# Pads between the SBUF tiles of the second block of an f32 transformer kernel on one Trainium2 core

## The chip, the core and the metric

The kernel runs on one core of a Trainium2 chip. Five engines share the work: TensorE (PE, matmuls; PEld is its loading of weights), VectorE (DVE), ScalarE (ACT), GpSimd (POOL) and SyncE (SP, which issues most DMAs). Tiles lie in SBUF, 128 partitions wide; a tile's place is one byte address, the same in each partition. Matmul results go to PSUM. The metric is the device time of one execution in microseconds (us); smaller is better.

## What is computed

Two blocks, one after the other, on 512 tokens with 1024 features, all in f32. The first (modulated norms, a gated delta rule, a window attention, a mixture of 32 experts) is not touched by the change. The second is:

```python
f = swiglu(rms_norm_2(h, ffn1_norm_pre), ffn1_w_gate, ffn1_w_up, ffn1_w_down)   # 1024 -> 2816 -> 1024
h = h + 0.5 * rms_norm_2(f, ffn1_norm_post)

proj = rms_norm_2(h, mix_norm_pre) @ w_in            # q, k, v (12 heads of 128), xr, yr, gates
q, k, v, xr, yr, gl = jnp.split(proj, splits, axis=-1)
attn = ...    # three dilated window attentions, merged by their log-sum-exp
rec = rg_lru_branch(xr, ...) * jax.nn.gelu(yr)       # conv of width 4, gates, a scan over the tokens
gates = jax.nn.sigmoid(gl).reshape(B, S, 2, D_MODEL)
merged = gates[:, :, 0] * (attn @ w_attn_branch) + gates[:, :, 1] * (rec @ w_rec_branch)
h = h + rms_norm_2(merged @ w_out, mix_norm_post)

f = swiglu(rms_norm_2(h, ffn2_norm_pre), ffn2_w_gate, ffn2_w_up, ffn2_w_down)
h = h + 0.5 * rms_norm_2(f, ffn2_norm_post)
```

## The kernel before

Activations are kept transposed: features on the partitions, the 512 tokens along a partition, so eight tiles of 2 KB per partition (`x0` to `x7`) hold all 1024 features. A projection `W^T x` gives 128 features at a time: eight k-tiles of weights, 128x128 each (512 bytes per partition, one after the other in one weight tile of 4 KB), against the eight activation tiles.

A large product is made of three f32r products. Each operand is split into a head of few bits and an exact rest, `h + l`, and `mm3` (L262 to L270) adds W_h x_h, W_h x_l and W_l x_h in PSUM:

```python
for i, k in enumerate(kts):
    w1, w2 = wh[:, i * P:(i + 1) * P], wl[:, i * P:(i + 1) * P]
    mm(ps, w1, xh[k], ...)      # L268
    mm(ps, w1, xl[k], ...)      # L269
    mm(ps, w2, xh[k], ...)      # L270
```

So a weight tile means 24 matmuls, each with its own load of 128x128 weights and 512 columns of activations that stream through; the loads run beside the matmul before. Weights come raw from HBM (`wload`, tile `wraw`); `wsplit` makes the head `wh` on ScalarE (L255) and the rest `wl` on VectorE (L256). `wraw`, `wh` and `wl` have four buffers each in the pool `wp2`; a new load waits until TensorE has done with a buffer.

The second block (`block2`) runs in this order:

- `ffn`, twice (before and after the mixer): `enter` closes the layer before and makes the first projections by halves of the tokens (256 columns); then gate and up projections from `xh`/`xl` (512 columns); their results are split to `hh`/`hl` in the pool `f1` (`f2`) and go through the down projections; `close` makes the last projections, the first four with 512 columns, the last four by halves with 256. `posth` (L1546) is a small tile of gains at the start of that pool.
- `mixer2`: four rounds, each with nine projections for one head of each attention group, then one head of the recurrence (`lru`: products by `xh`/`xl`, and small ones by `ch`/`cl`), into which the steps of `attention` (fp32 matmuls on `f` tiles, `sc`, `pT`) are woven. Then the merge: gates from `xh`/`xl`, the attention branch from `ah`/`al`, the recurrent one from `f`/`rs` (L1782 on), and `close` with `mh`/`ml`.

The order of the instructions on each engine follows the program text and a few woven generators; no table sets it. A tile's address follows from the pools: a pool lays its tiles one behind the other in the order in which tags are first used, and pools stand on each other like a stack.

Of the kernel before, what the change touches and what calls it, by code (L numbers as in the profile page):

```python
# [16 lines left out]
PSUM = bass.MemoryType.PSUM  # L17
# [13 lines left out]
# --------------------------------------------------------------------------  # L31
# host side: layout of the inputs and constants that depend on shapes alone
# --------------------------------------------------------------------------
def _mt(w, cols=None):
    """[K, M] -> [M/128, 128 (k), K/128, 128 (m)]"""
    if cols is not None:
        w = w[:, cols]
    k, m = w.shape
    return np.ascontiguousarray(w.reshape(k // P, P, m // P, P).transpose(2, 1, 0, 3))


def _cols(v):
    """[n*128] -> [128, n]"""
    return np.ascontiguousarray(np.asarray(v).reshape(-1, P).T)


def layout(a):
# [39 lines left out]
    # block 2  # L87
# [23 lines left out]
    def lru(n):  # L111
        w = a[n][0].reshape(4, 2, P, 2, P)  # head, k tile, k, m tile, m
        return w.transpose(2, 0, 3, 1, 4).reshape(P, 8 * 2 * P)
# [15 lines left out]
def constants():  # L129
# [8 lines left out]
    # [t, c]: t <= c / t > c inside a chunk  # L138
# [31 lines left out]
    # relative position: one-hot bucket rows and a mask row, over u  # L170
# [14 lines left out]
# --------------------------------------------------------------------------  # L185
# device side
# --------------------------------------------------------------------------
# [5 lines left out]
def weave(main, *fill):  # L193
    """the steps of main, and after each one `rate` steps of every filler (gen, rate)"""
    due = [0.0] * len(fill)
    for _ in main:
        for i, (gen, rate) in enumerate(fill):
            due[i] += rate
            while due[i] >= 1.0:
                due[i] -= 1.0  # L200
                next(gen, None)


class Net:
# [16 lines left out]
    def bt(self, shape, dt=F32):  # L221
        """a 2 KB per partition tile out of the shared set"""
        return self.t(self.bp, shape, "big", dt, bufs=self.nbig)
# [22 lines left out]
    # ---- weights: raw f32 -> 12-bit head (f32r) + exact rest (f32r)  # L246
# [11 lines left out]

    def weights(self, ap, n):
        return self.wsplit(self.wload(ap, n), n)  # L260

    def mm3(self, ps, wh, wl, xh, xl, kts, start=True, stop=True):  # L262
        """ps += W^T x over the k-tiles; wh/wl [128, nk*128]; xh/xl lists of [128, N]"""
# [8 lines left out]
    def mm3y(self, ps, wh, wl, xh, xl, kts, start=True, stop=True, n=3):  # L272
        """mm3 in steps of n k-tiles"""
# [10 lines left out]
    # ---- rsqrt of a small tile (x > 0), Newton on the vector engine  # L284
# [11 lines left out]
    # ---- softplus of a small tile  # L296
# [20 lines left out]
    # ---- 1/rms over the features of a T-layout activation, broadcast to all partitions  # L317
    def sumsq(self, acc, k, src):
        """acc += src^2"""
# [7 lines left out]
    def sumsq2(self, acc, k, src, hs):  # L327
        """acc[:, hs] += src[:, hs]^2, without the tensor engine or the vector engine"""
# [7 lines left out]
    def rstd_half(self, hf, *accs):  # L336
        """[P, 2]: 1/rms of the tokens of a half; the sums over the features on the tensor engine"""
# [36 lines left out]
    # ---------------------------------------------------------------- block 1  # L374
    def ada(self, items, raws=None):
        """mod[:, g] = w_ada^T silu(c) + b_ada by halves: the k-tiles as moving operand in four column tiles"""
# [49 lines left out]
    def block1(self):  # L426
# [39 lines left out]
        # statistics of x  # L466
# [5 lines left out]
        # scale1, shift1 by halves; k-tiles 0..3 of the projections of k follow the first halves  # L472
# [50 lines left out]
        # conv + silu (twice the value)  # L523
# [14 lines left out]
        def stats2(src, pst, base):  # L538
            """pst[:, i, base:base+2] = per token sums of squares over the two 64-halves"""
# [10 lines left out]
        # ---- gates  # L550
        def gates():
            # four k-tiles beside each other in the columns of the array
# [23 lines left out]
        def decays():  # L576
# [4 lines left out]
            # sum over a chunk, per head on the partitions of its half  # L581
# [12 lines left out]
        # ---- k: token major, normalised, and back  # L594
# [32 lines left out]
        # ---- decay and -M, its transpose  # L627
# [30 lines left out]
        # ---- q, v  # L658
# [11 lines left out]
        # ---- attention inside chunks, transposed, over k  # L670
# [19 lines left out]
        # ---- projections of the window attention  # L690
# [46 lines left out]
        # ---- sliding window attention  # L737
# [59 lines left out]
        # ---- z  # L797
# [7 lines left out]
        # ---- (I + M)^-1 by doubling of the diagonal blocks  # L805
# [46 lines left out]
        # ---- scaled v and k, token major, behind the inverse  # L852
        vb, kd, nw = MT, kt, [None] * 4

        def uw():
# [11 lines left out]
            for i in range(4):  # L867
# [3 lines left out]
                # -w^T [d (head parity), pair, chunk parity * 64]  # L871
# [11 lines left out]
        # ---- scan over the chunks; o = s o', s = rq / 8: s rsqrt(s^2 mean(o'^2) + eps)  # L883
# [62 lines left out]
        # results of the experts: rows for the first and the second expert of a token  # L946
# [7 lines left out]
        # ---- output projection: the rows of the window attention, then those of the delta rule  # L954
# [14 lines left out]
        # router: logits = (x * rstd * gain + shift) W = rstd * (x (gain W)) + shift W  # L969
# [34 lines left out]
    # ------------------------------------------------- block 1: mixture of experts  # L1004
    def moe(self):
# [5 lines left out]
        # the pairs of one group at a distance: its experts tend to be in demand together  # L1011
        order = [4 * g + i for i in range(4) for g in range(4)]
        NP = NE // 2
        # the results of the last pairs go to x by the tensor engine, the others by DRAM
        NL = 2

        def load(n, part=(0, 1)):
            """weights of pair n: gate | up in two halves per expert, down"""
# [15 lines left out]
        # slots beyond the last token keep finite values  # L1034
# [4 lines left out]
        # ---- normalized tokens, token-major, and a copy in DRAM  # L1039
# [13 lines left out]
        # ---- routing  # L1053
# [3 lines left out]
        def first_max(l, n, tag):  # L1057
            """the maximum, one-hot of its first place"""
# [24 lines left out]
        # [tok, tile, expert]  # L1083
# [10 lines left out]
        # tokens of the same expert before a token: in its tile, and in the tiles before (last: all)  # L1094
# [7 lines left out]
        # place of a token at its experts, from 1  # L1102
# [9 lines left out]
        # weights of the two experts  # L1112
# [20 lines left out]
        # pair: token, weights at its two experts, rows of the results  # L1133
# [6 lines left out]
        # tiles of the passes beyond the first  # L1140
        q1, q2, q3, q4 = (self.t(self.tp, [P, S], "cy" if q < 2 else "th") for q in range(4))
        # (no reuse of an index that a transfer may still read)
# [3 lines left out]
        def oindex(p, r):  # L1146
            """place of a slot's row in yd, or its token (the last pairs); its token"""
# [14 lines left out]
        def select(p, r):  # L1162
            """slots 64r..64r+63 of the two experts of the p-th pair: one-hot by token; token and weight of a slot"""
# [19 lines left out]
        def gather(p, r):  # L1183
            """their tokens, one on a partition"""
# [8 lines left out]
        def feed(xTs, hf, pt):  # L1193
            """gain and shift of the tokens, features on the partitions"""
# [19 lines left out]
        def pick(oh):  # L1214
            """the same by the tensor engine, without the way through DRAM"""
# [11 lines left out]
        def piece(p, c, o, r):  # L1227
            """512 columns of the weights of an expert of pair p"""
# [30 lines left out]
        def expert2(p, hT, idx, wv, r=0):  # L1259
            """weighted results, to DRAM; of the last pairs: in two parts, with the one-hot of the tokens by slot"""  # L1260
# [23 lines left out]
        def combine(ys, hs):  # L1284
            """x += gate * the results of the slots, at their tokens"""
# [13 lines left out]
        def ahead(p):  # L1299
            """the passes of pair p beyond the first: tokens fetched early"""  # L1300
# [11 lines left out]
        def more(p):  # L1312
            """the second and third pass of pair p"""
# [9 lines left out]
        def rest(p, r=3):  # L1323
            """the passes beyond, with weights loaded again"""
# [5 lines left out]
        def fetch(i):  # L1330
            """the results in DRAM for the tokens of a tile"""
# [5 lines left out]
        def collect(i, y):  # L1337
            """x += gate * the results in DRAM"""
# [51 lines left out]
    def headmm(self, aT, bT, i):  # L1390
        """[c, h, s] = sum_d a[d, c] b[d, s] for the two chunks of pair i; even heads, odd heads"""
# [24 lines left out]
    # ---------------------------------------------------------------- block 2  # L1416
    def bias_tables(self):
        """rows of the relative bias (with the mask), repeated in DRAM to be read back skewed"""
# [20 lines left out]
    def bias_load(self, dst, j, p):  # L1439
        """dst [128, 512]: group 0 (256 keys), group 1, group 2 (128 keys of the phase)"""  # L1440
# [9 lines left out]
    def halfsplit(self, h, l, src):  # L1450
        """h + l = src / 2"""
# [3 lines left out]
    def addnorm(self, k, f, pb, gcol, hs):  # L1455
        """x += f * gain / rms(f) for a half of the tokens (pb: 1/rms, in PSUM)"""
# [4 lines left out]
    def close(self, f, aps, xh, xl, evac):  # L1461
        """the last projections of a layer, f[m] = evac(W[m]^T x); the last four of them by halves of the tokens"""
# [27 lines left out]
    def enter(self, aps, gcol, post=None):  # L1490
        """the end of a layer (post: its result, 1/rms of the halves and gain) and the first projections of the next:
        xh + xl = x * gcol; returns the projections with the weights aps and 1/rms of x, broadcast"""
# [47 lines left out]
    def ffn(self, wgu, wd, pre, postg, post, fp):  # L1540
        """the projections down; returns what enter() needs to close the layer"""
# [3 lines left out]
        ph = self.t(fp, [P, KT], "posth")  # L1545
# [39 lines left out]
    def attention(self, j, q, k, vt, ap2, o):  # L1585
        """the p phases of head j, in steps"""
# [61 lines left out]
    def lru(self, rb, lp, rec):  # L1648
        """the gated recurrence, a head after the other, in steps"""
        nc, v, s = self.nc, self.nc.vector, self.nc.scalar  # L1650
        A, c2 = self.A, self.cols2
        cb, bx, ba, apar = (c2[:, 8 * i:8 * i + 8] for i in (6, 7, 8, 9))
        convw = self.const("convw2", [P, KT, 4], pool=lp)
# [8 lines left out]
        def head(h):  # L1662
# [17 lines left out]
            for q in range(2):  # L1680
                # twice gelu(yr)
# [43 lines left out]
    def mixer2(self, post):  # L1725
# [3 lines left out]
        with tc.tile_pool(name="mx", bufs=1, reuse_waits="tile") as mx:  # L1729
            att = [self.t(mx, [P, S], f"rs{k}") for k in range(4)]  # L1730
            rec = [self.t(mx, [P, S], f"rs{k + 4}") for k in range(KT)]
            with tc.tile_pool(name="at", bufs=1, reuse_waits="tile") as ap2:
                head = self.lru(rb, ap2, rec)
                for j in range(4):
# [27 lines left out]
            with tc.tile_pool(name="mg", bufs=1, reuse_waits="tile") as gp:  # L1762
                ah = [self.t(gp, [P, S], f"ah{k}", F32R) for k in range(4)]
                rh = [self.t(self.ap, [P, S], f"f{k}", F32R) for k in range(KT)]
                # a rest takes the place of the result before it
# [54 lines left out]
    def build(self):  # L1820
# [6 lines left out]
        with ExitStack() as st:  # L1827
# [31 lines left out]
            with ExitStack() as s1:  # L1859
# [5 lines left out]
                self.wp = pool(s1, "wp2", 4, reuse_waits="tile")  # L1865
                self.nsplit = 4
# [22 lines left out]
```

## Time and profile before

| | before |
|---|---|
| runs, median of 3 | 2241.49 us (2240.81 to 2242.68) |
| profiled execution, span from first to last instruction | 2238.9 us |
| TensorE busy | 2095.0 us, 94% |
| VectorE busy | 1078.0 us, 48% |
| ScalarE busy | 718.2 us, 32% |
| GpSimd busy | 202.9 us, 9% |
| second block | 857 to 2239 us of the span |

Of the profiled execution the page gives the span, not its time as a run; the span stands 2.6 us below the median of the runs. A matmul's record lasts longer than the distance to the next one's start, because matmuls are pipelined; a run's rate is read from the starts. Rows of the trace carry the names of the tiles without buffer numbers: `mm<-xh,wh` is a matmul into the PSUM tile `mm` with the moving operand `xh` and the weights `wh`.

### The profile page before, as it was taken

How to read it: one execution, taken by the hardware profiler on the slowest of the kernel's cores; microseconds unless marked ns; L12 is line 12 of the kernel's file. 1: busy time of each engine (PE TensorE's matmuls, PEld its weight loads, DVE VectorE, ACT ScalarE, POOL GpSimd, SP SyncE). 2: the span in 40 equal slices, each digit the busy share in tenths (PEclk: the TensorE clock that was granted, in tenths of full speed). 3: DMA queues.
4: the chain of work that ended last, by engine and by line, in shares of the span. 5: the costliest groups of instructions: out<-in, count | busy, mean ns of one | idle time of the engine just before them, and what ended most of it. 6: DMA issues, size and time to landing. Idle time of an engine off the chain costs nothing.

```text
span 2238.9 us, 32214 instructions
## 1 busy us (share of the span) xinstructions
PE 2095.0 (94%) x12908; PEld 1567.7 (70%) x12908; DVE 1078.0 (48%) x2071; ACT 718.2 (32%) x1197; POOL 202.9 (9%) x223
## 2 busy tenths in 40 slices
PE   5999999788888978999999899999999999999996
PEld 3677677553333427888888787878878888888886
DVE  4663655542221227553354864746564447542444
ACT  3432442122222224322222443525452243222221
POOL 3020002011111122000001300000000031000002
PEclk9999999788999988999999999999999999999998
DMA  7343315075968962323332232323222322233321
GB/s 262 112 133 105 105 48 160 29 284 215 399 238 329 382 249 95 99 90 91 102 92 82 88 83 76 113 67 113 62 99 90 108 76 81 93 89 95 98 90 38
DMA packets 93877, 294.53 MB, mean 132 GB/s; under 512 B 15746, under 2 KB 27010, under 8 KB 81404
## 3 DMA queue, kind: packets, MB, share of 16 engines
q1 hardware_dynamic: 86364, 278.03, 36.4%
q0 software_dynamic: 7328, 14.01, 1.9%
q8 instruction: 119, 1.95, 0.4%
q14 instruction: 66, 0.54, 0.1%
HBM read 286.12 MB, written 20.23 MB: 137 GB/s over the span
## 4 chain that ended last, share of the span: by engine, by line
PE 57%; DVE 3%; POOL 1%; ACT 1%; issue 1%; POOLq 0%; ACTq 0%; DVEq 0%
PE mm L269 18%; PE mm L270 18%; PE mm L268 18%; PE sm L1605 1%; DVE xl L1507 1%; PE mm L1633 1%; POOL x L1459 1%; POOL ss L334 1%; DVE cy L1458 0%; PE mm L1630 0%; ACT wh L255 0%; PE sm L1620 0%; PE sm L1757 0%; PE mm L1289 0%; PE sm L1603 0%
## 5 line engine op out<-in xcount | busy, mean ns | idle before, releaser
L268 PE MATMUL mm<-xh,wh 128*128 128x512 f32 (+1 forms) x1584 | 621.4, 395 | 8.4 <-ACT xh L1506 4.1
L269 PE MATMUL mm<-xl,wh 128*128 128x512 f32 (+1 forms) x1584 | 612.4, 387 | 4.0 <-DVE xl L1507 4.0
L270 PE MATMUL mm<-xh,wl 128*128 128x512 f32 (+1 forms) x1584 | 609.7, 386 | 0.1
L255 ACT ACTIVATE wh<-wraw 128x1024 fp32r<-128x1024 f32 (+3 forms) x282 | 274.1, 974 | 771.8 <-PE mm L269 681.4
L256 DVE TENSOR_TENSOR wl<-wraw,wh 128x1024 fp32r<-128x1024 f32 (+3 forms) x282 | 315.0, 1118 | 196.6 <-ACT wh L255 191.3
L268 PEld LDWEIGHTS mm<-xh,wh 128*128 128x128 f32 x1584 | 301.4, 191 | 81.5 <-issue 8.3
L269 PEld LDWEIGHTS mm<-xl,wh 128*128 128x128 f32 x1584 | 303.1, 191 | 66.1 <-DVE xl L1507 5.7
L270 PEld LDWEIGHTS mm<-xh,wl 128*128 128x128 f32 x1584 | 302.6, 191 | 62.9 <-issue 1.2
L334 POOL TENSOR_TENSOR ss<-ss,sq 128x256 f32<-128x256 f32 (+1 forms) x69 | 66.9, 970 | 951.6 <-ACT sq L333 935.5
L268 PE MATMUL mm<-hh,wh 128*128 128x512 f32 (+1 forms) x416 | 149.8, 360 | 0.0
L270 PE MATMUL mm<-hh,wl 128*128 128x512 f32 (+1 forms) x416 | 149.6, 360 | 0.0
L269 PE MATMUL mm<-hl,wh 128*128 128x512 f32 (+1 forms) x416 | 149.4, 359 | 0.0
L1241 PE MATMUL mm<-wmoe,xgT 128*64 128x512 f32 x512 | 128.5, 659 | 8.1 <-issue 8.1
L1241 PEld LDWEIGHTS mm<-wmoe,xgT 128*64 128x64 f32 x512 | 42.8, 152 | 83.8 <-issue 76.4
L268 PEld LDWEIGHTS mm<-hh,wh 128*128 128x128 f32 x416 | 78.1, 188 | 13.3
L269 PEld LDWEIGHTS mm<-hl,wh 128*128 128x128 f32 x416 | 78.1, 188 | 13.3
L270 PEld LDWEIGHTS mm<-hh,wl 128*128 128x128 f32 x416 | 78.0, 188 | 13.2
L1567 DVE TENSOR_TENSOR sq<-mm,rsb 128x512 f32<-128x512 f32 x44 | 30.4, 691 | 110.7 <-PE mm L270 110.7
L1562 DVE TENSOR_TENSOR cy<-mm,rsb 128x512 f32<-128x512 f32 x44 | 30.4, 691 | 91.6 <-PE mm L270 89.6
L1247 DVE SCALAR_TENSOR_TENSOR mth<-mth,mm 128x256 f32<-128x256 f32 x16 | 6.7, 420 | 114.3 <-ACT mth L1246 114.3
L1275 PE MATMUL mm<-wmoe,hT 128*64 128x512 f32 x256 | 57.9, 592 | 0.0
L1198 ACT ACTIVATE xgT<-mm,mod,gs 128x128 f32<-128x128 f32 x64 | 27.9, 462 | 77.4 <-DVE xgT L1200 69.8
(495 smaller groups left out, 2613.7 us busy)
## 6 DMA issues: line engine op xcount, KB each, us to landing
wmoe<-in_wmoe SPq DMA_DIRECT2D x96, 1024.0 KB
wraw<-in_win SPq DMA_DIRECT2D x90, 512.0 KB
wraw<-in_wgu SPq DMA_DIRECT2D x88, 512.0 KB
wraw<-in_wada SPq DMA_DIRECT2D x32, 512.0 KB
wraw<-in_wd SPq DMA_DIRECT2D x32, 448.0 KB
big<-in_wada SPq DMA_DIRECT2D x16, 512.0 KB
wraw<-in_wd SPq DMA_DIRECT2D x16, 512.0 KB
wraw<-in_wout SPq DMA_DIRECT2D x16, 256.0 KB
```

What stands on the lines that cost most here:

```text
L255: self.nc.scalar.activation(h[:, :n], raw[:, :n], AF.Copy)
L256: self.nc.vector.tensor_sub(l[:, :n], raw[:, :n], h[:, :n])
L268: mm(ps, w1, xh[k], start=start and i == 0, stop=False)
L269: mm(ps, w1, xl[k], start=False, stop=False)
L270: mm(ps, w2, xh[k], start=False, stop=stop and i == nk - 1)
L334: self.nc.gpsimd.tensor_add(acc[:, hs], acc[:, hs], sq[:, hs])
L1198: s.activation(xTs[hf][:, k, :], pt[:, k, :], AF.Identity, scale=self.gs2[:, kk:kk + 1], bias=mod[:, 3, kk:kk + 1])
L1241: mm(pg_[cs, :], xT[k // 4][:, k % 4, cs], piece(p, c, k // 4 * 2048 + k % 4 * S, r), start=k == 0, stop=k == KT - 1)
L1275: mm(py[cs, :], hT[:, k, cs], piece(p, c, 4096 + k * 1024 + n * S, r), start=k == 0, stop=k == 1)
L1459: (self.nc.gpsimd if k % 2 else self.nc.vector).tensor_add(self.x[k][:, hs], self.x[k][:, hs], t[:, hs])
L1562: v.tensor_mul(t1, pp[0], rb)
L1567: v.tensor_mul(t2, pp[1], rb)
```

## The change

A helper `even` takes a tile that nothing writes or reads, and so moves what the pool lays down after it. It is called at three places, and `posth` grows from 32 to 512 bytes per partition. Otherwise only comments go, which moves line numbers by a few.

```diff
+    def even(self, pool, nbytes):
+
+        self.t(pool, [P, nbytes // 4], "pad", bufs=1)
...
     def ffn(self, wgu, wd, pre, postg, post, fp):
...
-        ph = self.t(fp, [P, KT], "posth")
+        ph = self.t(fp, [P, P], "posth")[:, 0:KT]
         v.tensor_scalar_mul(ph, postg, 0.5)
...
     def lru(self, rb, lp, rec):
...
+        self.even(lp, 384)
         convw = self.const("convw2", [P, KT, 4], pool=lp)
...
             with tc.tile_pool(name="at", bufs=1, reuse_waits="tile") as ap2:
                 head = self.lru(rb, ap2, rec)
+                self.even(ap2, 64)
...
                 self.wp = pool(s1, "wp2", 4, reuse_waits="tile")
+                self.even(self.wp, 480)
                 self.nsplit = 4
                 self.block2()
```

The addresses that the two built programs give to the operands of f32r products, modulo 512 bytes:

| products | columns | weights before | activations before | weights after | activations after |
|---|---|---|---|---|---|
| first block, `xh`/`xl` | 512 | 128 | 128 | 128 | 128 |
| second block, `xh`/`xl` | 512, 256 | 32 | 0 | 0 | 0 |
| `hh`/`hl` | 512, 256 | 32 | 64 | 0 | 0 |
| `ch`/`cl` | 512 | 32 | 96 | 0 | 448 |
| `ah`/`al` | 512 | 32 | 32 | 0 | 0 |
| `f` / `rs` (heads / rests) | 512 | 32 | 0 / 32 | 0 | 0 / 0 |
| `mh`/`ml` | 512, 256 | 32 | 32 | 0 | 0 |

Of the attention's fp32 operands, `pT` goes from 96 to 448 and `sc` from 480 to 320. The instructions of every engine stand in the same order in both programs, and as many of them. One wait is new: the instruction that writes `posth` in the first `ffn` waits for a queue of weight loads, at the count of a load of expert weights whose buffer the larger `posth` now shares. The first block and the experts keep their addresses.

## Rows read from the trace of the kernel before

**Rows 1.** The page: busy time by engine; chain that ended last, by line.
```profile
PE 2095.0 (94%) x12908; PEld 1567.7 (70%) x12908; DVE 1078.0 (48%) x2071; ACT 718.2 (32%) x1197; POOL 202.9 (9%) x223
...
PE mm L269 18%; PE mm L270 18%; PE mm L268 18%; PE sm L1605 1%; DVE xl L1507 1%; PE mm L1633 1%; POOL x L1459 1%; POOL ss L334 1%; DVE cy L1458 0%; PE mm L1630 0%; ACT wh L255 0%; PE sm L1620 0%; PE sm L1757 0%; PE mm L1289 0%; PE sm L1603 0%
```

**Rows 2.** Windows: us, busy of PE, PEld, DVE, ACT, POOL; clock, DMA share, GB/s.
```profile
857.00:1232.00 375.00, 373.75 (x1775) 309.27 (x1776) 174.37 (x245) 112.75 (x151) 18.43 (x16) 0.99 0.31 95
1232.00:1850.00 618.00, 605.84 (x3078) 498.85 (x3078) 347.12 (x568) 247.93 (x395) 44.01 (x60) 0.99 0.29 88
1850.00:2239.00 389.00, 368.51 (x1723) 302.62 (x1721) 179.64 (x269) 107.69 (x145) 24.36 (x27) 0.97 0.27 84
```

**Rows 3.** Chain of waits from 889 to 1019 us, by line.
```profile
by line: PE mm L268 33.4%; PE mm L269 33.4%; PE mm L270 33.4%
```

**Rows 4.** Timeline, TensorE, first and last of 561 products: start, duration, line, tiles.
```profile
888.93 0.40 PE L268 MATMUL mm<-xh,wh 128*128 128x512 f32 x1
...
1019.59 0.40 PE L270 MATMUL mm<-xh,wl 128*128 128x512 f32 x1
```

**Rows 5.** Timeline, TensorE, first and last of 96 products with mh, ml.
```profile
1785.59 0.40 PE L268 MATMUL mm<-mh,wh 128*128 128x512 f32 x1
...
1807.16 0.39 PE L270 MATMUL mm<-mh,wl 128*128 128x512 f32 x1
```

**Rows 6.** Timeline, TensorE, first block, first and last of 44 products.
```profile
66.19 0.39 PE L269 MATMUL mm<-xl,wh 128*128 128x512 f32 x1
...
75.94 0.39 PE L270 MATMUL mm<-xh,wl 128*128 128x512 f32 x1
```

**Rows 7.** Groups by line and shape, 857 to 2239 us: busy us, mean ns, idle.
```profile
L268 PE MATMUL mm<-xh,wh 128*128 128x512 f32 x1152 | 459.5, 399 | 0.0
...
L268 PE MATMUL mm<-hh,wh 128*128 128x512 f32 x288 | 113.8, 395 | 0.0
...
L268 PE MATMUL mm<-xh,wh 128*128 128x256 f32 x192 | 56.1, 307 | 7.3 <-ACT xh L1506 4.1 <-ACT wh L255 3.1
L268 PE MATMUL mm<-hh,wh 128*128 128x256 f32 x128 | 36.0, 281 | 0.0
...
L269 PE MATMUL mm<-ml,wh 128*128 128x512 f32 x32 | 12.5, 389 | 0.0
```

**Rows 8.** One line's view of L1546; timeline of the last expert's down products.
```profile
L1546 DVE TENSOR_SCALAR posth<-c_cols x2: 156/156/156, 872.2 to 1843.3; 128x8 f32<-128x8 f32 x2
...
834.32 3.65 PE L1275 MATMUL mm<-wmoe,hT 128*64 128x512 f32 x16
```

**Rows 9.** Timeline, TensorE, mixer, first and last of 71 products.
```profile
1282.77 0.39 PE L270 MATMUL mm<-xh,wl 128*128 128x512 f32 x1
...
1299.09 0.40 PE L268 MATMUL mm<-xh,wh 128*128 128x512 f32 x1
```

**Rows 10.** Timeline, TensorE, first block after a break: second, sixth and ninth product.
```profile
127.33 0.40 PE L269 MATMUL mm<-xl,wh 128*128 128x512 f32 x1
...
128.26 0.39 PE L270 MATMUL mm<-xh,wl 128*128 128x512 f32 x1
...
128.94 0.39 PE L270 MATMUL mm<-xh,wl 128*128 128x512 f32 x1
```

**Rows 11.** Timeline, TensorE, 256 columns: first and last of 120, mh then hh.
```profile
1807.39 0.28 PE L268 MATMUL mm<-mh,wh 128*128 128x256 f32 x1
...
1821.66 0.28 PE L270 MATMUL mm<-mh,wl 128*128 128x256 f32 x1
...
2195.39 0.28 PE L268 MATMUL mm<-hh,wh 128*128 128x256 f32 x1
...
2209.27 0.28 PE L270 MATMUL mm<-hh,wl 128*128 128x256 f32 x1
```

**Rows 12.** Groups from 889 to 1019 us: the two halves of the weight split.
```profile
L256 DVE TENSOR_TENSOR wl<-wraw,wh 128x1024 fp32r<-128x1024 f32 x20 | 24.4, 1221 | 1.8 <-ACT wh L255 1.8
L255 ACT ACTIVATE wh<-wraw 128x1024 fp32r<-128x1024 f32 x20 | 21.2, 1060 | 63.8 <-PE mm L269 63.7
```

## Prediction

> **What bounds the kernel now.** The page comes first. TensorE is busy for 94% of the span and no other engine for more than half of it; in the chain that ended last, three lines, the three products of `mm3`, make up more than half of the whole [rows 1]. Next, the second block by stages: first feed-forward layer, mixer, second feed-forward layer, 1382 us in all, with TensorE busy for 1348.1 of them at a mean granted clock of 0.97 to 0.99 [rows 2]. Then the chain inside a stretch of a feed-forward layer, 889 to 1019 us: TensorE alone, a third for each of the three lines [rows 3]. Whatever brings two products closer together there shortens the run by as much.
>
> A matmul's own duration is no measure of that, since the next one starts before it ends. So I take the first and the last row of an unbroken run. From 888.93 to 1019.59 us, 561 products `xh`/`xl` of 512 columns follow each other: 130.66 us over 560 gaps is 233.3 ns [rows 4]. From 1785.59 to 1807.16 us, 96 products `mh`/`ml` of the same shape: 21.57 us over 95 gaps is 227.1 ns [rows 5], start included. The table of offsets tells the two apart: weights and activations are 32 bytes apart (modulo 512) in the first run and at the same offset in the second. A third run is in the first block, where the same kind of tile `xh`/`xl` stands at offset 128 and its weights at 128: 44 products from 66.19 to 75.94 us, 9.75 us over 43 gaps, 226.7 ns [rows 6]. So the gap is 227 ns in two cases and 233 in one, they differ as the change's words say, and the two with 227 are at different offsets (32 and 128), in two regions of the memory, with two kinds of tile. `hh`, 32 bytes off to the other side, has the mean of the case with 233, 395 ns, against 389 for `ml` [rows 7].
>
> **The change part by part.** It adds no instruction and moves none; addresses change, and one wait is added. That *wait* is on the semaphore of one weight-load queue, ahead of `posth` (L1546) of the first feed-forward layer, at 872.2 us. It is for a load of expert weights which the last expert's down products also wait for, and those start at 834.32 us [rows 8], 38 us before. Queued behind `posth` on VectorE are the rest of the rsqrt for `r`, which TensorE's spread waits for, and weight splits; they stand no longer than before. Cost 0; the load can't be later than the products that used it.
>
> *512 columns in the feed-forward layers.* Each layer shows uncut runs of 561 and 384 products by `xh` and 336 and 96 by `hh`: 1377, in two layers 2754. From 233.3 to a settled 226.7 is 6.6 ns each: 2754 x 6.6 = **18.2 us**.
>
> *512 columns in the mixer.* Of the 3456 products by `xh`/`xl` (3 lines x 1152 [rows 7]) 2 x 945 were in the layers above; 1566 are left. 1061 of them stand in 17 runs of 48 to 76, such as the 71 from 1282.77 to 1299.09 us: 16.32 us over 70 gaps, 233.1 ns [rows 9]. The other 505 stand in pieces between the attention's small products. There the start of a run matters: after a break in the first block, at equal offsets, four gaps come to (128.26 - 127.33) / 4 = 232.5 ns, and only then three to (128.94 - 128.26) / 3 = 226.7 [rows 10]. With six such gaps at a start, 1061 x 6.6 less 17 x 6 x 6 ns is 7.0 - 0.6 = **6.4 us**; for the 505 in pieces I take 2 ns each, **1.0 us**, between 0 (never settled) and 3.3 us (always). The 216 products by `f` and `rs` (two thirds of them 32 bytes apart) I take at the same 6.6 ns less a fifth, 216 x 5.3 = **1.1 us**, between 0 and 1.4. `ah`, `mh` and `ml` are equal before and after: 0.
>
> *256 columns.* Here the sign turns. At equal offsets, 120 products by `mh` from 1807.39 to 1821.66 us have 119.9 ns a gap; 120 by `hh`, 32 bytes apart, from 2195.39 to 2209.27 us have 116.6 [rows 11]. The change makes `hh` and `xh` equal: 384 of `hh` (3 x 128 [rows 7]) lose up to 3.3 ns, I take 2.9, since a few gaps around breaks are longer already: 1.1 us. 576 of `xh` (3 x 192 [rows 7]) lose between 0 (waits in their stretches hide it) and 3.3 ns; I take 1.7, the middle: 1.0 us. Together **-2.1 us**.
>
> *What stays unequal.* `ch`/`cl` go from 64 bytes on one side to 64 on the other, 96 products; by the distance of the two cases that is 6.6 ns either way, 0.6 us; I take 0, since 32 bytes gave the same on both sides. The attention's fp32 products with `pT` and `sc` change offsets too, about 200 of them; the nearest price is again 6.6 ns either way, 1.3 us; I take 0.
>
> *Does TensorE stay the bound?* A weight tile's 24 products will take 5.44 us instead of 5.60. ScalarE and VectorE need 1.06 and 1.22 us for a tile, and ScalarE idles 63.8 us of 130 until TensorE gives a buffer back [rows 12]; the DMA engines are busy for 0.31 [rows 2]. Nothing else comes due.
>
> Sum: 18.2 + 6.4 + 1.0 + 1.1 - 2.1 = 24.6 us. The profiled execution, of which the page has the span alone, is 2238.9 us long, so it would be 2214.3; the median of the runs is 2241.5, 2.6 us (0.1%) more than that span, and the same saving gives **2216.9 us**, 1.1% less.
>
> [...] In the rows, products start every 226.7 ns at equal offsets and every 233.3 at unequal ones [rows 4, 6]. [...]
>
> **The rivals.**
> *A: the offset is not the cause.* Something else that `mh` and the first block share makes them fast, and the same tiles stay at 233.3 ns: no change, 2239 to 2244 us. For it: no row has the same tile at both offsets in the same stage. Against it: three cases with one common trait, and no gap of 227 without it. That the pads miss their goal belongs here; the table of offsets excludes it for all but `ch`/`cl`. 6%. [...]
> *B: it holds in the uncut runs alone.* In the mixer each step of the attention sets the settling back, and nothing is won there: 18.2 - 2.1 = 16.1 us, 2225.4. For it: the longer gaps at a start [rows 10]. Against: two thirds of the mixer's products are in long runs, as uncut as those of the layers [rows 9]. 12%.
> *C: slower, by the place zero.* Both cases with 227 ns stand at 32 and 128; after the change weights and activations both start at offset 0, which no row shows. If the two reads then meet at every start, each product of 512 columns pays on top of 233.3 ns what equality costs at 256 columns, 3.3 ns [rows 11]: (2754 + 1566 + 216) x 3.3 = 15.0, with the 2.1 above 17.1 us, 2258.6. The change turns slower once the new gap is over 233.3 - 2.1 us / 4536 = 232.8 ns. Against it: 32 and 128 differ as much from each other, and gave the same. 4%.
>
> **How the numbers follow.** Forecast 78%, B 12%, A 6%, C 4%. With 6.6 ns everywhere, no loss at starts and no price at 256 columns, 4536 x 6.6 = 29.9 us would be won, 2211.6; with 1.9 us for the terms that I took at 0, the low end is 2210. The high end takes in B, 2225.4, rounded up to 2226. Outside are A, C and some 8% of the rest. Faster by over 0.2% (4.5 us, about what a measurement of this kernel can tell from no change): forecast and B, 0.90; within it A, 0.06; slower C, 0.04.
>
> **What would show it.** Uncut runs of `xh` and `hh` at 226.7 to 227.1 ns by first and last row; their means down from 395 to 389; `hh` with 256 columns up to 120 ns a gap; the first feed-forward layer about 9 us shorter, the mixer about 8, the first block as it was; as many instructions as before; no idle time at `posth`. Wrong would be a gap of `xh` still at 233 ns (A, or C if above), a mixer as long as before (B), or a shorter gap with a span that stays, which would mean that weights come late.

## Result, and the profile after

The changed kernel takes 2217.56 us (median of 4 runs, 2215.8 to 2218.51) against 2242.09 us for the kernel before (4 runs, 2240.81 to 2243.88). The ratio is 0.9893, with a 95% interval of 0.988 to 0.9906. The forecast was 2216.9 us. The profiled execution is a run of 2215.8 us with a span of 2214.0 us.

The page of the changed kernel, busy time by engine, answers to [rows 1]: as many instructions on every engine, TensorE still busy for 94%, 22 us less of it.

```profile
PE 2072.9 (94%) x12908; PEld 1569.1 (71%) x12908; DVE 1075.8 (49%) x2071; ACT 718.0 (32%) x1197; POOL 203.4 (9%) x223
```

Timeline of TensorE after the change: first and last product of the run of 561 by `xh`/`xl`, of the run of 96 by `mh`/`ml`, and of the 120 by `hh`/`hl` with 256 columns (line numbers are four higher than before).

```profile
890.77 0.39 PE L272 MATMUL mm<-xh,wh 128*128 128x512 f32 x1
...
1017.73 0.39 PE L274 MATMUL mm<-xh,wl 128*128 128x512 f32 x1
...
1770.08 0.39 PE L272 MATMUL mm<-mh,wh 128*128 128x512 f32 x1
...
1791.61 0.39 PE L274 MATMUL mm<-mh,wl 128*128 128x512 f32 x1
...
2169.39 0.28 PE L272 MATMUL mm<-hh,wh 128*128 128x256 f32 x1
...
2183.66 0.28 PE L274 MATMUL mm<-hh,wl 128*128 128x256 f32 x1
```

The run that had 233.3 ns a gap [rows 4] has 126.96 us over 560 gaps, 226.7 ns. `mh`, equal before and after, keeps its place: 21.53 us over 95 gaps, 226.6 [rows 5]. `hh` with 256 columns went the other way, from 116.6 [rows 11] to 14.27 us / 119 = 119.9.

Groups after the change, 857 to 2214 us (busy us, mean ns of one, idle before), against [rows 7]: 399 to 393 for `xh`, 395 to 389 for `hh`, and 281 to 285 for `hh` with 256 columns.

```profile
L272 PE MATMUL mm<-xh,wh 128*128 128x512 f32 x1152 | 453.0, 393 | 0.0
...
L272 PE MATMUL mm<-hh,wh 128*128 128x512 f32 x288 | 112.0, 389 | 0.0
...
L272 PE MATMUL mm<-hh,wh 128*128 128x256 f32 x128 | 36.5, 285 | 0.0
```

Where the time went is read by setting the two timelines side by side. Both have the same products in the same order, so each stage can be measured from its first product to the next stage's first product:

| stretch of the span (us) | before | after | difference | forecast |
|---|---|---|---|---|
| start to the first product of the second block | 857.26 | 859.11 | +1.85 | 0 |
| entry of the first feed-forward layer, 256 columns | 27.74 | 27.72 | -0.02 | |
| its products with 512 columns | 325.22 | 316.09 | -9.13 | -9.1 |
| its close and the entry of the mixer, 256 columns | 58.12 | 58.46 | +0.34 | |
| mixer and merge, 512 columns | 539.05 | 530.46 | -8.59 | -8.5 |
| close of the mixer, entry of the second layer, 256 columns | 62.81 | 61.51 | -1.30 | |
| second layer, 512 columns | 325.19 | 316.04 | -9.15 | -9.1 |
| last close and the end, 256 columns | 43.51 | 44.60 | +1.09 | |
| the four stretches with 256 columns together | 192.18 | 192.29 | +0.11 | +2.1 |
| span | 2238.90 | 2213.99 | -24.91 | -24.6 |

In the last stretch 0.61 of the 1.09 us lie in the 192 products; the other 0.48 lie behind the last product, and what makes them was not looked into. Within the run of 561 and the run of 96 the granted clock is 1.00 after the change as it was before (the windows of before stand in the last section), so it is no cause of the shorter gaps. Windows after: time, busy time of TensorE, granted clock, DMA share, GB/s.

```profile
891.00:1017.70 126.70, 126.70 (x560) 1.00 0.29 95
1770.10:1791.60 21.50, 21.50 (x96) 1.00 0.29 97
```

### The profile page after: what moved, and what is told of

It is laid out like the page before. It is cut to its first block, busy times and chain, and to the rows that moved or that the text cites. A ratio compares the mean times of both kernels' runs of the same rounds, so it can differ in the third digit from the quotient of the medians.

```text
span 2214.0 us, 32214 instructions
## 1 busy us (share of the span) xinstructions
PE 2072.9 (94%) x12908; PEld 1569.1 (71%) x12908; DVE 1075.8 (49%) x2071; ACT 718.0 (32%) x1197; POOL 203.4 (9%) x223
## 3 DMA queue, kind: packets, MB, share of 16 engines
q0 software_dynamic: 7328, 14.01, 1.9%
## 5 line engine op out<-in xcount | busy, mean ns | idle before, releaser
L272 PE MATMUL mm<-xh,wh 128*128 128x512 f32 (+1 forms) x1584 | 614.4, 390 | 8.3 <-ACT xh L1510 4.5
L273 PE MATMUL mm<-xl,wh 128*128 128x512 f32 (+1 forms) x1584 | 604.7, 382 | 4.4 <-DVE xl L1511 4.2
L274 PE MATMUL mm<-xh,wl 128*128 128x512 f32 (+1 forms) x1584 | 602.1, 381 | 0.0
```

Of the source, the lines that this page charges most:

```text
L272: mm(ps, w1, xh[k], start=start and i == 0, stop=False)
L273: mm(ps, w1, xl[k], start=False, stop=False)
L274: mm(ps, w2, xh[k], start=False, stop=stop and i == nk - 1)
```

## Experiments

All kernels are edits of the changed one; `...` in an edit marks code left out. Two theories were to be told apart: that the distance between weights and activations, modulo 512 bytes, sets the gap, or that the place of either does. Gaps below are taken from the first and last row of a run, as above. "Second block" is the time from its first product to the end of the span: 1381.64 us before, 1354.88 after.

### The weights' pad alone

```diff
-        ph = self.t(fp, [P, P], "posth")[:, 0:KT]
+        ph = self.t(fp, [P, KT], "posth")
...
-        self.even(lp, 384)
...
-                self.even(ap2, 64)
```

> Only the 480-byte pad ahead of the weight tiles: weights at offset 0, xh/xl at 0 (equal), f/rs equal, hh/hl at 32 (still 32 bytes apart). Theory (the gap between two f32r products depends on whether weights and activations stand at the same offset modulo 512): xh runs at 226.7 ns, hh runs of 512 columns at 233.3, hh of 256 columns at 116.6; the saving of the whole change, 24.5 us, less 864 x 6.6 - 384 x 2.9 = 4.6 us for hh, so 2222 us. Rival (the pads act through something else, such as where the weight tiles lie in memory): hh speeds up with the weights, 2217.5 us, or nothing does, 2242 us.

Measured: 2222.13 us (median of 4 runs, 2217.03 to 2227.12), ratio 0.9902 (0.9874 to 0.993). First and last row of the 561 products by `xh`, and of the 336 by `hh` behind them:

```profile
895.82 0.39 PE L272 MATMUL mm<-xh,wh 128*128 128x512 f32 x1
...
1022.78 0.39 PE L274 MATMUL mm<-xh,wl 128*128 128x512 f32 x1
1023.01 0.40 PE L272 MATMUL mm<-hh,wh 128*128 128x512 f32 x1
...
1101.18 0.40 PE L274 MATMUL mm<-hh,wl 128*128 128x512 f32 x1
```

126.96 us over 560 gaps is 226.7 ns; 78.17 us over 335 is 233.3. The weights have moved for both, and only the pair that became equal is faster. The second block takes 1361.17 us, 20.5 less than before, where 19.9 was expected.

### The larger `posth` alone

```diff
-        self.even(lp, 384)
...
-                self.even(ap2, 64)
...
-                self.even(self.wp, 480)
```

> Only the larger posth: hh/hl go from 64 to 32, where the weights still are (32, equal); xh/xl stay at 0 (32 apart). Theory: hh at 226.7 ns with 512 columns and 120 with 256, xh unchanged at 233.3; saving 4.6 us, 2237.5 us. Rival (place zero or the place of the weights does it): no change, 2242 us.

Measured: 2234.4 us, ratio 0.9966 (0.995 to 0.9981). The same two runs:

```profile
886.26 0.40 PE L272 MATMUL mm<-xh,wh 128*128 128x512 f32 x1
...
1016.91 0.40 PE L274 MATMUL mm<-xh,wl 128*128 128x512 f32 x1
1017.15 0.40 PE L272 MATMUL mm<-hh,wh 128*128 128x512 f32 x1
...
1093.09 0.39 PE L274 MATMUL mm<-hh,wl 128*128 128x512 f32 x1
```

Now it is `hh` that has 226.7 ns (75.94 us / 335) and `xh` 233.3 (130.65 / 560), with weights that did not move at all. The second block takes 1376.62 us, 5.0 less than before, as expected; the profile's first block happened to end 2.7 us earlier than before's, and the median is 3 us under the expectation. The two parts add up to 25.5 us of the 26.8 that the second block gained in the profile of the whole change; 1.0 of the other 1.3 lies in the entry of the second layer, of which more below.

### Everything 96 bytes further

```diff
                 self.cols2 = self.const("cols2", [P, 80], pool=self.ap)
+                self.even(self.ap, 96)
```

> All pads of the change and 96 bytes more ahead of xh: weights and activations of the second block all at offset 96 instead of 0. Theory (equality decides, not the place): 226.7 ns as with the change, 2217.5 us. Rival (offset 0, a whole multiple of 512, is what helps): 233.3 ns for all, 2242 us or more.

Measured: 2215.0 us, ratio 0.9878 (0.9847 to 0.9909), 226.7 ns in the runs by `xh` (126.98 us / 560) and by `hh`, second block 1354.84 us. First and last row of the 561 by `xh`:

```profile
890.91 0.39 PE L272 MATMUL mm<-xh,wh 128*128 128x512 f32 x1
...
1017.89 0.39 PE L274 MATMUL mm<-xh,wl 128*128 128x512 f32 x1
```

Place zero has no part in it; rival C of the prediction falls, and so does A, since the same tiles in the same stage have now been seen at equal and at unequal offsets.

### Other distances: is it 512?

```diff
-        ph = self.t(fp, [P, P], "posth")[:, 0:KT]
+        ph = self.t(fp, [P, 160], "posth")[:, 0:KT]
...
+                self.even(gp, 64)
                 mh = [self.t(gp, [P, S], f"mh{k}", F32R) for k in range(KT)]
...
-                self.even(self.wp, 480)
+                self.even(self.wp, 736)
```

> Three distances in one run: weights at 256, xh/xl at 0 (256 apart), hh/hl at 384 (128 apart), mh/ml at 320 (64 apart). Theory (equal modulo 512 and nothing less): 233.3 ns for all three at 512 columns, 116.6 at 256 columns, time as before the change, 2242 us. Rival (a smaller modulus, 256, 128 or 64, is enough): 226.7 ns for xh alone, for xh and hh, or for all three; 2222, 2218 or 2217 us.

Measured: 2223.03 us (one run). The theory's "nothing less than 512" is wrong. The run of 561 by `xh`, 256 bytes apart, and the run of 336 by `hh`, 128 apart:

```profile
891.51 0.39 PE L272 MATMUL mm<-xh,wh 128*128 128x512 f32 x1
...
1018.47 0.39 PE L274 MATMUL mm<-xh,wl 128*128 128x512 f32 x1
1018.70 0.40 PE L272 MATMUL mm<-hh,wh 128*128 128x512 f32 x1
...
1096.86 0.39 PE L274 MATMUL mm<-hh,wl 128*128 128x512 f32 x1
```

`xh` has 226.7 ns (126.96 us / 560), as at distance 0; `hh` has 233.3 (78.16 / 335). So equality modulo 256 is enough in these runs. `mh`, 64 apart, has 229.1, a value between the two.

Four more kernels, then, with other pads, and in three of them with the weights 4 floats into a wider slot, so that distances finer than 32 bytes can be had. The edit to the slots (`off` is 4 there; the pads are as the expectations say):

```diff
-        h = self.t(self.wp, [P, 1024], "wh", F32R, bufs=self.nsplit)
-        l = self.t(self.wp, [P, 1024], "wl", F32R, bufs=self.nsplit)
+        wide = 1152 if self.nsplit == 4 else 1024
+        h = self.t(self.wp, [P, wide], "wh", F32R, bufs=self.nsplit)[:, off:off + 1024]
+        l = self.t(self.wp, [P, wide], "wl", F32R, bufs=self.nsplit)[:, off:off + 1024]
```

> Weight tiles start 16 bytes into a wider slot: weights at 16, xh/xl at 0 (16 apart), hh/hl at 96 (80 apart), mh/ml at 480 (48 to the other side). Theory (only a distance of 0 modulo 256 gives 226.7 ns, 64 something between): 233.3 ns for xh, 230 to 233.3 for hh and mh, time 2242 us or a few us less. Rival (the gap grows with the distance): xh near 228 ns, time near 2225 us.

> Weights at 96, xh/xl at 0 (96 to one side), hh/hl at 192 (96 to the other), mh/ml at 288 (192 apart, which modulo 256 is 64 to the other side than in scan1). Theory (distance modulo 256, same on both sides): xh and hh alike, 229 to 233.3 ns; mh 229 ns as at 64; time 2230 to 2242 us. Rival (the side matters): xh and hh differ, or mh is at 233.3 ns.

> Weights at 80, xh/xl at 0 (modulo 256 a distance of 176, which is 80 to one side), hh/hl at 128 (48 to the other), mh/ml at 192 (112). [...] Rival (some other distance is as good as equality or better): one of them at 226.7 ns or less.

> Weights at 112, xh/xl at 0 (144 modulo 256), hh/hl at 128 (16 to the other side than in scan16), mh/ml at 288 (176). [...] Rival: a distance at 226.7 ns or less.

Measured, one run each: 2227.15, 2239.16, 2237.24 and 2237.19 us. The gaps at 512 columns, by the distance of the activations ahead of the weights in the built programs, modulo 256 (`xh` run of 561, `hh` run of 336, `mh` run of 96):

| distance | gap, ns | seen in |
|---|---|---|
| 0 | 226.7 | `xh`, `hh`, `mh`, several kernels |
| 16 | 228.3 | `hh`, weights at 112 |
| 32 | 233.3 | `hh` before |
| 48 | 231.9 | `hh`, weights at 80 |
| 64 | 229.1 | `mh`, weights at 256 |
| 80 | 230.0 | `hh`, weights at 16 |
| 96, 112, 128, 144 | 233.3 to 233.4 | `hh`, `mh`, `hh`, `xh`; weights at 96, 80, 256, 112 |
| 160 | 234.3 | `xh`, weights at 96 |
| 176 | 232.0 | `xh`, weights at 80; `mh`, weights at 112 |
| 192, 208 | 233.3 | `mh`, `mh`; weights at 96, 16 |
| 224 | 233.3 | `xh` before |
| 240 | 226.7 or 233.3 | `xh`, weights at 16, by run |

None of the sixteen distances is below the gap of equality, so equality is the best of those tried. The side matters, against the theory put down for the second of the four kernels: 64 has 229.1 and 192 has 233.3, and 16 differs from 240. That modulo 256 is the right fold is seen twice: at 0 and 256, both with 226.7, and at 176, which is 432 modulo 512 for `xh` and 176 for `mh`, both with 232.0. The gap does not grow steadily with the distance, as the rival for the first kernel had it. Distance 240 was a surprise: the kernel with the weights at 16 has runs of either kind, with no instruction or address changed between them. Timeline of that kernel, the run of 561 by `xh`, and the run of 384 by the same tiles in the same layer:

```profile
889.58 0.39 PE L273 MATMUL mm<-xh,wh 128*128 128x512 f32 x1
...
1016.51 0.39 PE L275 MATMUL mm<-xh,wl 128*128 128x512 f32 x1
...
1094.03 0.39 PE L273 MATMUL mm<-xh,wh 128*128 128x512 f32 x1
...
1183.39 0.39 PE L275 MATMUL mm<-xh,wl 128*128 128x512 f32 x1
```

126.93 us over 560 gaps is 226.7 ns; 89.36 over 383 is 233.3. So a run of this kernel settles on one of two gaps and keeps it to its end, and the second feed-forward layer repeats the pattern of the first. What at the start of a run chooses was not tried; at 512 columns equality has shown one settled gap alone, 226.7 ns, in every run of 40 and more products.

### Equal for 512 columns, apart for 256

Since equality costs at 256 columns, two kernels put only the weight tiles that are used by halves off their place, by 8 floats (32 bytes) and by 16 (64 bytes), and pad the recurrence by 448 bytes, which makes `ch`/`cl` equal. The edit of the first, with the wider slot as above; the second has 16 in place of 8:

```diff
-        ws = [self.weights(aps[m], 1024) for m in range(4, KT)]
+        ws = [self.weights(aps[m], 1024, 8) for m in range(4, KT)]
...
-        w = [self.weights(ap, 1024) for ap in aps]
+        w = [self.weights(ap, 1024, 8) for ap in aps]
...
-        self.even(lp, 384)
+        self.even(lp, 448)
```

> As after the change, but the weight tiles that are used by halves of 256 columns alone (in enter and in the second half of close) start 32 bytes into a wider slot, and the recurrence's pad is 448 bytes, so that ch/cl are at 0 too. Theory (equality costs at 256 columns what it gives at 512): 512 columns stay at 226.7 ns; 256 columns go from 120 to 117 or 118: 384 x 2.9 + 576 x 1.7 + 192 x 2.5 = 2.6 us, 0.5 us for ch/cl, so 3 us less than with the change, 2214.5 us. Rival (the half stages are bound by VectorE and ScalarE, or the mix of offsets disturbs the runs that follow): the same time as with the change, 2217.5 us, or more.

> The changed kernel once more, on the same chip as split32: 2217.5 us by both theories; second block 27 us shorter than before, first block the same within its own spread of some us.

> As split32, but the weights of the half products stand 64 bytes into their slots, a distance of 192 modulo 256, at which mh with 256 columns ran at 113.5 ns in scan96. Theory (the distance sets the gap, and at 192 the half products take 113.5 ns): runs of 256 columns 6.4 ns a product shorter than with the change; where TensorE is the bound (hh and mh in close, 576 products) that is 3.7 us, in enter nothing (there TensorE waits); 512 columns stay at 226.7 ns; second block 1330.5 us by the trace against 1334.2, 2214 us if the first block takes as long as usual. Rival (113.5 ns came from something else about mh in that run): 118 ns as in split32, second block 1334 us.

Measured: 2218.04 us with 32 bytes (ratio 0.9891, 0.9875 to 0.9906) and 2220.1 for the changed kernel again on the same chip (0.99, 0.9885 to 0.9916); 2217.1 with 64 bytes (0.9884, 0.9863 to 0.9905). None can be told from another, and in the profiles the second block is as long in all three (1354.89, 1354.63 and 1354.66 us). The changed kernel's is 27.0 us shorter than before, as expected; the 3 us and the 3.7 us expected of the two edits were not won.

The gaps did fall: 120 products by `mh` with 256 columns take 118.3 and 117.7 ns (14.08 and 14.01 us / 119) instead of 119.9. The 113.4 ns that `mh` had once at the distance of 64 bytes to this side (192 modulo 256; 13.50 us / 119, in the kernel with the weights at 96) did not come back in these runs. Timeline, first and last of the 120, in that kernel and in the one with 64 bytes:

```profile
1806.28 0.28 PE L272 MATMUL mm<-mh,wh 128*128 128x256 f32 x1
...
1819.78 0.28 PE L274 MATMUL mm<-mh,wl 128*128 128x256 f32 x1
```
```profile
1793.78 0.28 PE L273 MATMUL mm<-mh,wh 128*128 128x256 f32 x1
...
1807.79 0.28 PE L275 MATMUL mm<-mh,wl 128*128 128x256 f32 x1
```

But it did come back elsewhere in the kernel with 64 bytes. The second half of the same close, at the same distance, settles on it, 3.06 us over 27 gaps, 113.3 ns:

```profile
1814.96 0.28 PE L275 MATMUL mm<-mh,wl 128*128 128x256 f32 x1
...
1818.02 0.28 PE L275 MATMUL mm<-mh,wl 128*128 128x256 f32 x1
```

So at 192 a run with 256 columns has settled on 117.7 or on 113.3 ns, as one with 512 columns at 240 on 226.7 or 233.3, and the distance alone does not set it. The expectation for 64 bytes, 113.5 ns throughout, fell: its second block, which it counts to the last product, takes 1334.0 us and not 1330.5. `hh`, 32 bytes apart, shows the same: before the change its 120 products in a close had 117.8 ns in the first layer and 116.6 in the second [rows 11], and 117.8 in both with the weights' pad alone.

The 192 products with 256 columns of the three closes are together 0.8 us (32 bytes) and 1.5 us (64 bytes) shorter than in the changed kernel. `ch`/`cl`, now equal, gained 0.2 us where 0.5 was expected (96 products to the next start: 23.5 us instead of 23.7). But the entry of the second layer took 1.2 to 1.3 us longer in both, and by the windows of that entry this goes with the granted clock. Window, busy time of TensorE, granted clock, DMA share, GB/s; before, after, 64 bytes:

```profile
1832.30:1870.20 37.90, 31.71 (x214) 0.86 0.18 57
```
```profile
1816.70:1853.30 36.60, 30.27 (x214) 0.91 0.16 53
```
```profile
1818.10:1856.00 37.90, 31.20 (x215) 0.86 0.18 54
```

In all thirteen traces this entry takes either 37.7 to 38.0 us at a mean clock of about 0.86 (six of them) or 36.4 to 36.8 at 0.91 (seven). TensorE idles there between its halves (30.27 us busy of the 36.6 after the change, 31.71 of 37.9 before), and for a part of it the granted clock is 0.50: from 1824.6 to 1831.2 us after the change, from 1841.4 to 1844.6 and from 1858.4 to 1865.1 before. The two groups do not follow the offsets: the kernel with the weights' pad alone has `xh` equal and the longer entry, two of those at unequal distances (144 and 176) have the shorter. What chooses was not tried. That is also where the 1.30 us of the table of stages came from, so they are no part of what equality gives.

## Why the prediction was right

**What bounds the kernel.** TensorE's gaps, as said: a saving of 6.6 ns a product came out of the span in full. The two layers' stretches with 512 columns are 9.13 and 9.15 us shorter, where 2754 x 6.6 = 18.2 us had been put down.

**The mixer.** 8.59 us against 6.4 + 1.0 + 1.1. Summed from each product's start to the next, the 17 long runs gave 6.6, the pieces 1.2 and `f` and `rs` 0.85 us, so the terms came near one by one and not only in their sum. Rival B, nothing won there, falls: runs of 71 and 76 have 226.8 to 227.2 ns after the change, start included. The terms put at 0 were small: `ch`/`cl` lost 0.2 us, the attention's fp32 products and the other small ones together 0.1.

**256 columns: the one term that was mis-sized.** For `hh` 1.1 us of loss was put down and 1.0 measured (+0.39 and +0.61 in the 192 products of each close); the first layer lost less because `hh` had 117.8 ns there before, where the prediction had read the run of the second layer alone. For `xh` 1.0 us was put down, the middle between 0 and 3.3 ns, and it should have been the low end: the entry of the first layer changed by -0.02 us and that of the mixer by -0.05. The 3.3 ns were `hh`'s price and too high for `xh`: the entry's one uncut run of 96 by `xh` takes 11.32 us before (873.20 to 884.52) and 11.48 after (874.86 to 886.34), 1.7 ns a gap. That even this does not show in the stretch fits the waits for `xh` and `xl` in it [rows 7], 7.3 us before and 7.2 after. The entry of the second layer gained 1.3 us with the clock, which no step foresaw. So the second block gained 26.8 us and not 24.6, and 1.3 of that is luck.

**The first block hides that.** Its instructions and the offsets of its f32r operands are the same in all kernels here, yet its profiled length ranges from 854.6 to 864.1 us. After the change it was 1.85 us longer, which brought the span to -24.9 and so close to the forecast by luck: the agreement to 0.7 us is better than the working deserved. The granted clock is part of that spread at most: over the first block its mean is 0.94 in the two shortest (854.6 and 854.7 us) and 0.93 in the longest (864.1), but also 0.93 in one of 858.8. The rest stays open.

**The wait and the supply of weights.** `posth` (L1550 now) has no idle time ahead of it, and ScalarE still waits for TensorE and not the other way round: 61.0 us idle in 125 us of the first layer's run by `xh`, against 63.8 in 130 before [rows 12]. Line view of L1550, and the group of the weight split from 892 to 1017 us:

```profile
L1550 DVE TENSOR_SCALAR posth<-c_cols x2: 155/156/157, 874.1 to 1827.7; 128x8 f32<-128x8 f32 x2
its engine sat idle before it (us, times) until:
```
```profile
L255 ACT ACTIVATE wh<-wraw 128x1024 fp32r<-128x1024 f32 x20 | 21.2, 1060 | 61.0 <-PE mm L273 61.0
```

**What the offset did.** By this case's runs the time between the starts of f32r products depends on where one operand stands against the other: with nothing but addresses changed, the 3790 gaps in the long runs of the layers and the mixer went from 233.3 to 226.8 ns on average. What makes it so, no run here shows.

**What the prediction did not see.** Modulo 512 was taken over from the change's words; 256 is enough (226.7 ns at a distance of 256). Rival A falls with the first three experiments, and C, the place zero, with the third. And one of the pads does nothing: the built program has `ch` at 64 without the recurrence's two pads and at 448 with them, so 384 of the 448 bytes arrive. Both pads ask the same pool for the one buffer of the tag `pad`, and the smaller fits into the larger. In the kernels with one pad of 448, `ch` is at 0.

## What to carry to other kernels

When one engine sets the end, take the time between the starts of two instructions from a long run, by its first and last row, and compare runs of the same shape elsewhere in the same kernel; a difference of 3% that no wait explains (233.3 against 226.7 ns here) may be a matter of addresses. For streams of f32r products with 512 columns, try weights and activations at the same offset modulo 256 bytes, which gave 226.7 ns in this kernel where other distances gave up to 234.3; look at the built addresses, since a pad can be swallowed by its pool, as 64 of the 448 bytes were here. With 256 columns equality was among the slowest offsets here, by at most 6.6 ns a product (119.9 against 113.3), and taking it away won nothing in time.

## What the runs showed of the hardware

- Two f32r products of 512 columns start 226.7 ns apart at best here, and the offset between weights and activations decides up to 7.6 ns more (234.3 at distance 160). The granted clock is 1.00 in such runs. At 512 columns the 226.7 ns of equality are the least of all distances tried. At 256 columns equality gives 119.9 ns, which is as much as any: distances 96, 112 and 144 have about 120 ns as well, the others settle on 113.3 to 118.7, and 16 and 176 on 120.0 in one run and less in another. Why the sign turns stays open; no other width was run. Windows of the kernel before, inside the run by `xh` and the one by `mh`: time, busy time of TensorE, granted clock, DMA share, GB/s.

```profile
889.00:1019.00 130.00, 130.00 (x559) 1.00 0.30 93
...
1785.60:1807.10 21.50, 21.50 (x96) 1.00 0.29 97
```

- After a break a run needs some products to settle, at equal offsets too: four gaps of 232.5 ns on average, then three of 226.7 [rows 10]. At one distance, 240, it settled on 226.7 or on 233.3 ns and stayed there.
